# Linear attention of a four-layer trunk: its six projections as seven products of halves each

## The chip, the cores and the metric

One core of a Trainium2 chip runs the kernel. The metric is the device time of one execution in microseconds, as the median of several runs. A core has TensorE (in the profile PE for matmuls, PEld for loading the stationary operand), VectorE (DVE), ScalarE (ACT), GpSimd (POOL) and SyncE (SP). Each takes its instructions in order. SP and POOL also issue the DMAs; only POOL issues those that add to what is already in SBUF.

## The reference, cut to what matters

The model has four layers (S5, linear attention, differential attention, S5) of width 1024 over 512 tokens, each followed by a feed-forward. The change touches the second layer's mixer:

```python
def gla_mixer(h, w_in, w_a2, b_a, norm_g, w_o):
    proj = h @ w_in                                   # 512 x 1024 @ 1024 x 3088
    q, k, v, g, a_lo = jnp.split(proj, [512, 1024, 2048, 3072], axis=-1)
    log_a = jax.nn.log_sigmoid((a_lo @ w_a2 + b_a).astype(f32)) / GLA_TEMP
    cum = jnp.cumsum(log_a.reshape(shp_k), axis=2)    # chunks of 64 tokens, 4 heads
    tot = cum[:, :, -1]
    k_dec = k * jnp.exp(tot[:, :, None] - cum)
    upd = jnp.einsum('bnchk,bnchv->bnhkv', k_dec, v)
    state = dec_c[..., None] * state + upd_c          # scan over 8 chunks
    o = jnp.einsum('bnchk,bnhkv->bnchv', q, states)
    o = o * lax.rsqrt(jnp.mean(o * o, axis=-1, keepdims=True) + NORM_EPS) * norm_g
    o = o * jax.nn.silu(g)
    return o @ w_o
```

`h` is the RMS norm of x; x + mixer goes on to the feed-forward. All is in float32.

## The kernel before, in words

**Products.** Every large product runs as three matmuls of 32-bit parts: an operand is split into a rounded high part (a cast on ScalarE, line 414) and the low rest (a subtraction on VectorE, line 422), and high x high, high x low and low x high are added (`mm3`, lines 442 to 444). A weight arrives by DMA in a buffer `wst` (three of them) and is split into `whl` (five).

**Feed-forward.** Its first product runs in blocks of 512 columns by a scheme of seven products of halves (`seven_block`): tokens and contraction are halved, sums of the quarters of the activations ("sides" 1, 2, 3, 4, and the plain quarters 11, 12, 22; class `Sides`) and of the weights (1, 21, 22, 3) are formed, and each product is 2 x 4 x 3 matmuls that are 256 wide (line 585). Products six, seven and four add to the PSUM bank of product one, and three to that of five, after ScalarE or VectorE has read what stands there; two has a bank of its own. Sums of weights are made by a DMA that adds (POOL) and by VectorE (line 678). The first two blocks of a layer, in which the sides are made too, follow a plan written out as a list of steps; for it the order of all engines is by hand (`hand_all`). Elsewhere only TensorE's order is by hand, the order of the program (`hand(PE)`), and the other engines' instructions are put in order by a scheduler, by the order of the program among those that it holds ready.

**Linear attention** (`gla`, line 1903). The activations come as `Left`: eight transposed tiles with high and low parts. The six projections of 512 columns are plain products with 512-wide matmuls: q by `gemm_a4`, then in this order v (first half), k, v (second half), gate (first half), gate (second half), each by `gemm_b`. A `gemm_b` takes four weight pieces of two 128-row tiles; between pieces it calls functions given in `between`. These hold the rest of the work: `decays` (four 512-wide matmuls z, then on ScalarE absolute value, exponential and logarithm, lines 1970 to 1972), `later` (suffix sums, line 1977, and their exponential), `totals` (32 matmuls with two columns, line 1984), and for each half `hf` of the heads and token tile `t` `updates` (line 2007, then VectorE makes two states for each of two heads, line 2017) and `readout` (line 2031, ScalarE's sums of squares, line 2037, a power on POOL, line 533, and the scaled output, line 2045). An update of tile t stands one piece ahead of its readout. `turned` transposes the gated output (line 2062) and splits it (lines 538, 539). The output projection adds to x (line 566) and hands the rows to the next norm (lines 94, 107, 116).

## Time and profile before

| | |
|---|---|
| median of 3 runs (lowest, highest) | 2259.85 us (2259.85, 2261.8) |
| the profiled execution: its time, its span | 2262.09 us, 2260.1 us |
| linear attention's own matmuls, first projection to next layer's first product | 579.5 to 800.5 us of the span |
| HBM read, mean over the span | 285.62 MB; 134 GB/s with what is written |

The profile comes from one execution with a recorder running; a mean duration of an instruction is not its spacing, since matmuls and also the other engines' instructions overlap a little with the next. "Idle before" names what released an engine. A row "L2007 PE MATMUL upd<-v,kd" reads: line 2007, TensorE, a matmul that writes `upd` from `v` and `kd`.

### The profile page before, as it was taken

The page shows a single profiled execution, that of the slowest core. Times are in us where ns is not written, and L with a number is a line of the kernel's source. Part 1 is how long each engine was busy: PE and PEld are TensorE (multiplying, and loading weights), DVE is VectorE, ACT ScalarE, POOL GpSimd, SP SyncE. Part 2 cuts the span into 40 slices and gives each one's busy share as a digit, 9 for nine tenths or more (in the row PEclk, how much of TensorE's full clock was granted, in tenths as well). Part 3 has the DMA queues.
Part 4 walks back from the last instruction along what each step waited for, and adds up shares of the span by engine and source line. Part 5 has one row for each costly group of instructions (what it writes and reads, how often), then busy time and mean ns, then how long its engine had stood idle before and what let it go on. Part 6 is the DMA issues. An engine that isn't in the chain of part 4 may idle for free.

```text
span 2260.1 us, 37368 instructions
## 1 busy us (share of the span) xinstructions
PE 2185.5 (97%) x14967; PEld 1957.2 (87%) x14967; DVE 1578.0 (70%) x2415; ACT 1111.5 (49%) x1777; POOL 318.1 (14%) x432
## 2 busy tenths in 40 slices
PE   6999999999999999999999999999999899999998
PEld 5888889989777799998988888989999788989997
DVE  9955878776535488777745676976766965957675
ACT  8534635444443356564435675644544234635443
POOL 4301141430000010100002231101000000101000
PEclk9999999999999999999999999999999999999999
DMA  4356666663322566665346465975641545766622
GB/s 90 63 172 167 163 169 174 174 179 94 106 75 69 150 157 178 180 174 153 94 142 149 96 154 136 242 207 138 177 95 56 145 154 149 197 167 158 169 75 75
DMA packets 295527, 319.92 MB, mean 142 GB/s; under 512 B 70141, under 2 KB 235289, under 8 KB 295226
## 3 DMA queue, kind: packets, MB, share of 16 engines
q1 hardware_dynamic: 232730, 235.79, 34.2%
q0 software_dynamic: 62624, 81.75, 19.4%
q8 instruction: 118, 1.93, 0.3%
q14 instruction: 55, 0.45, 0.1%
HBM read 285.62 MB, written 16.65 MB: 134 GB/s over the span
## 4 chain that ended last, share of the span: by engine, by line
PE 83%; DVE 7%; ACT 4%; issue 3%; DMA 2%; SPq 1%; POOL 0%; DVEq 0%; POOLq 0%; ACTq 0%
PE a L585 17%; PE acc L442 13%; PE acc L444 13%; PE acc L443 13%; PE c L585 9%; PE d L585 5%; PE y L1490 2%; DVE whl L422 2%; ACT whl L414 1%; PE op L2332 1%; PE s L2299 1%; PE tp L116 1%; PE V L1454 1%; PE acc L2387 1%; DMA wst<-in_ffn_w_down_dram 1%
## 5 line engine op out<-in xcount | busy, mean ns | idle before, releaser
L422 DVE TENSOR_TENSOR whl<-wst,whl 128x1024 fp32r<-128x1024 f32 x272 | 331.7, 1224 | 277.8 <-ACT whl L414 276.7
L414 ACT CAST whl<-wst 128x1024 fp32r<-128x1024 f32 x272 | 284.9, 1052 | 339.7 <-PE acc L444 250.3
L585 PE MATMUL a<-side,whl 128*128 128x256 f32 x3168 | 382.5, 277 | 7.7 <-DVE whl L422 6.0
L585 PEld LDWEIGHTS a<-side,whl 128*128 128x128 f32 x3168 | 369.4, 188 | 10.1 <-DVE whl L422 6.8
L442 PE MATMUL acc<-whl,act 128*128 128x512 f32 x704 | 276.1, 392 | 1.9 <-DVE g L629 1.8
L444 PE MATMUL acc<-whl,act 128*128 128x512 f32 x704 | 274.5, 390 | 0.0
L443 PE MATMUL acc<-whl,act 128*128 128x512 f32 x704 | 274.5, 390 | 0.0
L585 PE MATMUL c<-side,whl 128*128 128x256 f32 x2112 | 254.7, 277 | 3.8 <-DVE whl L422 3.8
L585 PEld LDWEIGHTS c<-side,whl 128*128 128x128 f32 x2112 | 246.6, 188 | 4.8 <-DVE whl L422 4.6
L422 DVE TENSOR_TENSOR whl<-slot,whl 128x1024 fp32r<-128x1024 f32 x105 | 127.8, 1222 | 66.3 <-ACT whl L414 66.2
L442 PEld LDWEIGHTS acc<-whl,act 128*128 128x128 f32 x704 | 132.1, 188 | 31.4 <-DVE g L629 2.7
L444 PEld LDWEIGHTS acc<-whl,act 128*128 128x128 f32 x704 | 132.2, 188 | 27.7
L443 PEld LDWEIGHTS acc<-whl,act 128*128 128x128 f32 x704 | 132.2, 188 | 26.2
L414 ACT CAST whl<-slot 128x1024 fp32r<-128x1024 f32 x105 | 110.0, 1053 | 90.8 <-PE acc L444 46.3
L585 PE MATMUL d<-sides,whl 128*128 128x256 f32 x1056 | 129.2, 278 | 2.5 <-ACT whl L414 2.5
L585 PE MATMUL a<-sides,whl 128*128 128x256 f32 x1056 | 129.1, 278 | 1.8 <-DVE whl L422 1.2
L442 PE MATMUL acc<-whl,hT 128*128 128x512 f32 x320 | 129.1, 403 | 0.0
L585 PEld LDWEIGHTS d<-sides,whl 128*128 128x128 f32 x1056 | 124.8, 188 | 3.3 <-ACT whl L414 3.3
L585 PEld LDWEIGHTS a<-sides,whl 128*128 128x128 f32 x1056 | 124.9, 188 | 3.1 <-DVE whl L422 1.4
L443 PE MATMUL acc<-whl,hT 128*128 128x512 f32 x320 | 125.9, 393 | 0.0
L444 PE MATMUL acc<-whl,hT 128*128 128x512 f32 x320 | 125.8, 393 | 0.0
L620 POOL DMA_DIRECT2D wst<-in_ffn_w_gate_up_dram x44 | 57.0, 1296 | 443.2 <-DMA wst<-in_ffn_w_gate_up_dram 178.0
(456 smaller groups left out, 3938.1 us busy)
## 6 DMA issues: line engine op xcount, KB each, us to landing
wst<-in_ffn_w_gate_up_dram SPq DMA_DIRECT2D x88, 512.0 KB, 4.5
wst<-in_ffn_w_down_dram SPq DMA_DIRECT2D x88, 512.0 KB, 4.6
slot<-in_ffn_w_gate_up_dram SPq DMA_DIRECT2D x69, 512.0 KB, 6.2
wst<-in_ffn_w_gate_up_dram POOLq DMA_DIRECT2D x44, 512.0 KB, 6.0
halves<-in_ffn_w_gate_up_dram SPq DMA_DIRECT2D x42, 512.0 KB, 5.6
wst<-in_s_w_glu_dram SPq DMA_DIRECT2D x32, 512.0 KB, 5.0
wst<-in_gla_w_in_dram SPq DMA_DIRECT2D x24, 512.0 KB, 3.6
wst<-in_diff_w_qkv_dram SPq DMA_DIRECT2D x24, 512.0 KB, 3.9
```

The source lines that it names most:

```text
L116: tr.nc.tensor.transpose(p[:, j], h[:, j * P : (j + 1) * P], tr.ident[:])
L414: self.last["high"] = self.nc.scalar.copy(hl[:, 0], w[:])
L422: self.last["low"] = self.nc.vector.tensor_tensor(hl[:, 1], w[:], hl[:, 0].bitcast(F32), op=ALU.subtract)
L442: mm(out, lh, rh, start=first, stop=False)
L443: mm(out, lh, rl, start=False, stop=False)
L444: self.last["mm"] = mm(out, ll, rh, start=False, stop=last)
L585: mm(o, hl[:, x, k, c], row(y, k), start=first and not (j or k or n), stop=k == 3 and n == 2, skip_group_check=True,)
L620: nc.gpsimd.dma_start(w[:], left.quarter(*plus, b), accum_op=ALU.add)
L1454: mm(V[kk][z][:, bs(b)], inm[:, z, bs(b)], U[:, bs(b)], start=True, stop=True)
L1490: mm(yb[:, b], q[:, j, b], om[:, j // 2, bs(b)], start=False, stop=j == 3)
L2299: nc.tensor.matmul(ss[m][:], qs[:, m, ts], ks[:, m, z], start=z == 0, stop=z == 1)
L2332: nc.tensor.matmul(op[:, 0], aT[:, kt], vall[0][:, kt, j * P : (j + 1) * P], start=kt == 0, stop=kt == 3)
```

## The change

The six projections run as six blocks of seven products. Blocks 0 and 1 (q, first half of v) follow a plan like that of the feed-forward, blocks 2 to 5 (k, second half of v, the two gate halves) the function `block`, in which the former `between` functions stand between products. q is turned as before (weights stationary); the other five have the activations stationary (`held`). Each result is put together out of quarters by ScalarE copies and VectorE sums (`Turned`, `Rows`). The first feed-forward ends with `Sides` in place of `Left`. x is written to DRAM in two parts, its SBUF room is lent as `work` (the low-rank tile, scratch and the states, kept now as a ring of three token tiles), and x is read back behind the last readout. `la` (the log decays) and the second half of v share a room, as do others. `planned` only carries the loop over a plan's steps. Lines left out are marked by "...".

```diff
+GLA_COLS = (0, 1024, 512, 1536, 2048, 2560)
...
-    def seven_product(self, row, w, bank, first, hl=None):
+    def seven_product(self, row, w, bank, first, hl=None, held=False):
...
+                    two = (row(x, k)[:, c], hl[:, y, k]) if held else (hl[:, x, k, c], row(y, k))
                     mm(
-                        o, hl[:, x, k, c], row(y, k), start=first and not (j or k or n),
-                        stop=k == 3 and n == 2, skip_group_check=True,
+                        o, *two, start=first and not (j or k or n), stop=k == 3 and n == 2, skip_group_check=True,
+    def seven_quarters(self, slots, left, b, held, out, dbank):
...
+        def load(name, q, half, plus=None, room=None):
+            if name in ("11", "3"):
+                W[name] = self.staged(left.quarter(q, half, b), 4, 256)
+            else:
+                W[name] = slots.pop(0) if room is None else room
+                if room is not None:
+                    lent.add(name)
+                nc.sync.dma_start(W[name][:], left.quarter(q, half, b))
+            if plus:
+                nc.gpsimd.dma_start(W[name][:], left.quarter(*plus, b), accum_op=ALU.add)
+        def done(name):
+            if name not in lent:
+                slots.append(W[name])
...
+        def one():
+            bank["a"] = self.acc("a")
+            product("11", "11", bank["a"], True)
+        def one_out():
+            out.copy(0, 0, bank["a"])
+        def two():
+            bank["d"] = dbank("d")
+            product("12", "21", bank["d"], True)
+        def two_out():
+            out.plus(0, 0, bank["d"])
+            out.done(0, 0)
+        def five():
+            bank["c"] = self.acc("c")
+            product("1", "1", bank["c"], True)
+        def five_out():
+            out.copy(1, 1, bank["c"])
+        def add(name):
+            v.tensor_tensor(W["1"][:], W["1"][:], W[name][:], op=ALU.add)
+            done(name) if name == "21" else None
+        def six():
+            product("2", "1", bank["a"], False)
+        def six_out():
+            out.copy(0, 1, bank["a"])
+        def seven():
+            product("3", "3", bank["a"], False)
+        def seven_out():
+            out.minus(1, 1, bank["a"])
+            out.done(1, 1)
+        def three():
+            product("4", "22", bank["c"], False)
+            done("22")
+        def three_out():
+            out.less(0, 1, bank["c"])
+            out.done(0, 1)
+        def four():
+            product("22", "1", bank["a"], False)
+            done("1")
+        def four_out():
+            out.copy(1, 0, bank["a"])
+            out.done(1, 0)
...
+                    if l == 0:
+                        nxt = Sides(self, after, None, i["gla_w_in"][0], lambda half, b: GLA_COLS[b] + half * 256)
...
+                                ahead=(lambda: self.gla_ahead(nxt)) if tail and l == 0 else None,
+                                middle=(lambda: nxt.total("3")) if tail and l == 0 else None)
...
+    def gla_ahead(self, left):
+        self.xkept = self.dp.tile([SEQ, D], F32, name="xgla")
+        left.ahead(2)
+        self.nc.gpsimd.dma_start(
+            self.xkept[:].rearrange("(t p) c -> p t c", p=P)[:, :, :512], self.x[:, :, :512]
+        )
     def gla(self, l, left, after):
...
+        xd = self.xkept[:].rearrange("(t p) c -> p t c", p=P)
+        with self.tc.tile_pool(name="gla", bufs=1, reuse_waits="tile") as p:
+            room = lambda tag, name: p.tile([P, 4, 512], F32, tag=tag, name=name)
+            lent = [room(tag, "lent") for tag in "AB"]
+            left.open(p, ("1", "2", "3"))
+            v0 = room("C", "v0")
+            left.open(p, ("4", "22"))
+            lent.append(room("D", "lent"))
+            qT = room("Q", "qT")
+            on = [None, room("N", "on1")]
+            ng = p.tile([P, D], F32, name="ng")
             mask = p.tile([P, P], F32, name="mask")
+            ind = p.tile([P, 2], F32, name="ind")
+            dec = p.tile([P, NT, 4, 2], F32, name="dec")
+            walr = p.tile([P, KT, 32], F32R, name="walr")
+            wals = p.tile([P, 4, 32], F32R, name="wals")
+            nf = p.tile([P, NT], F32, name="nf")
+            fac = left.r
...
+            class Rows:
+                def __init__(_, to, then=None):
+                    _.to, _.then = to, then
+                def each(_, th, half, ps):
+                    for j in range(2):
+                        t = 2 * th + j
+                        yield t, _.to[:, t, half * 256 : half * 256 + 256], ps[:, j * 256 : j * 256 + 256]
+                def copy(_, th, half, ps):
+                    for t, o, y in _.each(th, half, ps):
+                        nc.scalar.mul(o, y, fac[:, t : t + 1])
+                def stt(_, th, half, ps, f, op):
+                    for t, o, y in _.each(th, half, ps):
+                        v.scalar_tensor_tensor(o, y, f[:, t : t + 1], o, op0=ALU.mult, op1=op)
+                def plus(_, th, half, ps):
+                    _.stt(th, half, ps, fac, ALU.add)
+                def minus(_, th, half, ps):
+                    _.stt(th, half, ps, nf, ALU.add)
+                def less(_, th, half, ps):
+                    _.stt(th, half, ps, fac, ALU.subtract)
+                def done(_, th, half):
+                    if _.then:
+                        _.then(slice(2 * th, 2 * th + 2), slice(half * 256, half * 256 + 256))
+            whole = lambda y: y[:].rearrange("p a b -> p (a b)")
+            parts = [whole(y)[:, n : n + 1024].rearrange("p (k n) -> p k n", n=256) for y in lent for n in (0, 1024)]
+            slots = [left.g[:].rearrange("p (k n) -> p k n", n=256)]
+            f = [
+                self.seven_quarters(slots, left, 0, False, Turned(), self.sbank),
+                self.seven_quarters(slots, left, 1, True, Rows(v0), self.sbank),
+            ]
+            f[0]["room21"](parts[0])
+            f[0]["room1"](parts[1])
+            f[1]["room21"](parts[2])
+            f[1]["room1"](parts[3])
+            f[0]["room22"](parts[4])
+            f[0]["summed"]()
+            f[1]["summed"]()
+            f[1]["room22"](parts[5])
+            wal = self.wp.tile([P, KT + 4, 16], F32, tag="wst", name="wal", bufs=3)
+            nc.sync.dma_start(wal[:, :KT], w[:, 3072:3088].rearrange("(a p) n -> p a n", p=P))
+            nc.sync.dma_start(ng[:], i["gla_norm"][0].partition_broadcast(P))
+            nc.gpsimd.dma_start(xd[:, :, 512:], self.x[:, :, 512:])
...
+            plan = """
+                split21a one:a split21b square flush one:b total1 one_out:a finish high1 low1 total2 split1a high2 low2
+                negative one_out:b two:a two:b split1b high3 two_out:a five:a add22a highSa two_out:b lowSa five_out:a
+                five:b add22b highSb diag lowSb low3 split3a six:a spread five_out:b rows six:b six_out:a split3b seven:a
+                six_out:b total4 split22a high4 low4 seven:b seven_out:a split22b three:a seven_out:b gates
+                add21a high22 low22 three:b highFa add21b lowFa highFb lowFb four:a four:b three_out:a three_out:b
+                four_out:a four_out:b
+            """
+            more = {"square": lambda: left.square(NT - 1, 1), "flush": self.flush, "gates": gates, "negative": negative}
+            self.planned(plan, left, f, more)
...
+            self.hand(mybir.EngineType.PE)
+            work = self.xp.tile([P, NT, D], F32, tag="x", name="work")
+            flat = whole(work)
+            aT, wa2 = flat[:, :512], flat[:, 512:1024]
+            ring = flat[:, :3072].rearrange("p (s z c n) -> p s z c n", s=3, z=2, c=2)
+            turn = [0]
+            def T():
+                turn[0] += 1
+                return flat[:, 3072 + turn[0] % 2 * 512 :][:, :512]
...
+            ap_ = self.sbank("alo")
+            sums = [(walr[:, k], "11" if k < 4 else "12", k % 4) for k in range(KT)]
+            sums = [sums, [(walr[:, k], "1", k) for k in range(4)] + [(wals[:, k], "22", k) for k in range(4)]]
+            for th in range(2):
+                for n, (a, side, k) in enumerate(sums[th]):
+                    for z in range(2):
+                        nc.tensor.matmul(
+                            ap_[:32, th * 256 : th * 256 + 256], a, left.row(side, z, k),
+                            start=not (th or n or z), stop=n == KT - 1 and z == 1, skip_group_check=True,
+                        )
+            v.tensor_tensor(aT[:32], ap_[:32], R[:32], op=ALU.mult)
             for h in range(4):
+                v.scalar_tensor_tensor(qT[:, h], qT[:, h], 128.0 ** -0.5, R[:], op0=ALU.mult, op1=ALU.mult)
+            kd = room("A", "kd")
+            on[0] = room("B", "on0")
+            la = room("D", "la")
...
-                    nc.scalar.activation(kd[:, t], row(bank), AF.Exp, scale=1.0 / 16.0)
+                    e = T()
+                    nc.scalar.activation(e, row(bank), AF.Exp, scale=1.0 / 16.0)
+                    v.tensor_tensor(kd[:, t], kd[:, t], e, op=ALU.mult)
...
+            vs = [v0, None]
+            st = lambda hf, z, ch: ring[:, (4 * hf + ch // 2) % 3, z, ch % 2]
...
+            def block(b, out, between):
+                between = iter(between)
+                s = self.seven_quarters(slots, left, b, True, out, self.acc)
+                for y in ("direct", "room1", "room22", "room21", "summed"):
+                    s[y]()
+                def step(*names):
+                    for n in names:
+                        s[n]()
+                    next(between, lambda: None)()
+                step("one", "one_out")
+                step("five", "five_out")
+                s["add"]("22")
+                step("six", "six_out")
+                step("two", "two_out")
+                step("seven", "seven_out")
+                step("three", "three_out")
+                s["add"]("21")
+                step("four", "four_out")
+            def gated(hf, gs):
+                def then(ts, cs):
+                    nc.scalar.activation(gs[:, ts, cs], gs[:, ts, cs], AF.Silu)
+                    v.tensor_tensor(on[hf][:, ts, cs], on[hf][:, ts, cs], gs[:, ts, cs], op=ALU.mult)
+                return Rows(gs, then)
             def core(hf):
-                def after0():
-                    if hf:
-                        readout(0, 3)
-                    updates(hf, 0)
-                def after1():
-                    readout(hf, 0)
-                    updates(hf, 1)
-                def after2():
-                    readout(hf, 1)
-                    updates(hf, 2)
-                def after3():
-                    readout(hf, 2)
-                    updates(hf, 3)
-                return after0, after1, after2, after3
+                steps = [lambda: updates(hf, 0)]
+                for t in range(3):
+                    steps.append(lambda t=t: (readout(hf, t), updates(hf, t + 1)))
+                return steps + [lambda: readout(hf, 3)]
+            slots += left.freed()
             pause = lambda: None
-            values(0, (decays, pause, pause, later))
-            self.gemm_b(stat, w, KT, 512, evac_k, between=(totals,))
-            values(1, core(0))
-            part = lambda hf, z: oT[hf][:, z] if hf == 0 else oT[1][z][:].bitcast(F32R)
-            gated(0, core(1))
-            g = self.gain(after)
-            first = lambda: (readout(1, 3), turned(0, (0,)))
-            gated(1, (first, *(lambda t=t: turned(0, (t,)) for t in (1, 2, 3))))
-            oT[1] = [late("oT1"), late("oT1")]
+            block(2, Rows(kd), (decays, pause, pause, pause, pause, totals))
+            vs[1] = room("D", "v1")
+            block(3, Rows(vs[1]), (later, *core(0)))
+            g = []
+            block(4, gated(0, room("C", "gate0")), core(1))
+            self.x = self.xp.tile([P, NT, D], F32, tag="x", name="x")
+            nc.gpsimd.dma_start(self.x[:], xd)
+            oT = [[room("D", "oT0"), room("A", "oT0")], None]
+            part = lambda hf, z: oT[hf][z][:].bitcast(F32R)
+            turns = [pause] + [lambda t=t: turned(0, (t,)) for t in range(NT)]
+            block(5, gated(1, room("C", "gate1")), turns)
+            oT[1] = [room("Q", "oT1"), room("B", "oT1")]
```

187 lines of the change are left out of this document (97 added, 90 removed).

## The prediction

> **What bounds the kernel now.** First the page: TensorE is busy for nearly the whole span, and the chain that ended last is mostly TensorE.
>
> ```profile
> span 2260.1 us, 37368 instructions
> PE 2185.5 (97%) x14967; PEld 1957.2 (87%) x14967; DVE 1578.0 (70%) x2415; ACT 1111.5 (49%) x1777; POOL 318.1 (14%) x432
> ...
> PE 83%; DVE 7%; ACT 4%; issue 3%; DMA 2%; SPq 1%; POOL 0%; DVEq 0%; POOLq 0%; ACTq 0%
> ```
>
> The change works in one stage, the linear attention (about 579 to 801 us). There I asked for the waits of TensorE and then for its engines by stretch (columns: PE, PEld, DVE, ACT, POOL busy, clock, DMA share, GB/s).
>
> ```profile
> PE acc L444 <- DVE oT L539: 1.0, 2, 0.7
> PE tp L116 <- DVE hh L94: 0.8, 1, 0.8
> ```
> ```profile
> 612.00:635.00 23.00, 23.00 (x89) 16.39 (x88) 6.35 (x7) 22.69 (x28) 0.00 (x0) 1.00 0.12 31
> 676.00:700.00 24.00, 24.00 (x128) 17.19 (x128) 11.21 (x24) 8.92 (x20) 2.09 (x3) 1.00 0.22 66
> ```
>
> TensorE waits 1.8 us in 222: it alone sets the time, and only fewer matmul columns shorten the stage. But two helpers are nearly unused (VectorE 11.2 of 24 us), while ScalarE is full from 612 to 635 (22.69 of 23). That costs nothing now, because TensorE has 22 us of products that ask nothing of ScalarE. Whether this stays so is the question.
>
> **The products (removed work).** A 512-wide matmul of line 442 to 444 starts every 0.227 us: 24 of them lie between the first row and the third. A 256-wide product of 24 matmuls (line 585) takes 2.72 us, from start to start of the last two rows.
>
> ```profile
> 606.38 0.39 PE L442 MATMUL acc<-whl,hT 128*128 128x512 f32 x1
> ...
> 611.83 3.60 PE L1968 MATMUL z<-wa,aT 128*128 128x512 f32 x8
> 614.87 0.80 PE L442 MATMUL acc<-whl,hT 128*128 128x512 f32 x1
> ```
> ```profile
> 877.50 2.88 PE L585 MATMUL c<-side,whl 128*128 128x256 f32 x24
> 880.22 2.88 PE L585 MATMUL a<-side,whl 128*128 128x256 f32 x24
> ```
>
> (611.83 - 606.38) / 24 = 0.227; half as wide, 2.72 / 24 = 0.1133, exactly half. Before, one 512-column projection is 8 x 4 x 3 = 96 wide matmuls, 21.8 us. After, it is 7 x 24 = 168 narrow ones, 19.04 us. Six projections: 6 x 2.72 = **-16.3 us**. The low-rank matmuls keep their columns (16 wide become 32 narrow). [...]
>
> **The head, written out by hand.** Blocks 0 and 1 (q and the first half of v) run by a copy of the feed-forward's opening plan, which the trace has for the layer after: one wait in its 14 products.
>
> ```profile
> 836.91 5.50 PE L585 MATMUL a<-side,whl 128*128 128x256 f32 x46 [1.73 <-DVE whl L422]
> ```
> ```profile
> 441.40:460.60 19.20, 19.20 (x171) 19.20 (x170) 16.22 (x19) 11.29 (x15) 1.29 (x1) 1.00 0.67 174
> ```
>
> Here VectorE leaves out that plan's two gate scalings, so I take **+0.5 us**, bounds 0 and twice the row, 3.5. The weights now come in 7 loads of 512 KB per block instead of 4. The second row is such a block of the first feed-forward, also with five weight slots: TensorE has no gap there at 174 GB/s, so the loads are hidden. The half of x that POOL writes to DRAM stands ahead of the sums of blocks 0 and 1 in POOL's fixed order and waits for x; the other half stands ahead of the norm's power but is ready before it. I price both, and the reading back during block 5 (due only after block 5 and half an output projection, over 40 us), at nothing; uncovered, 2 MB at the 174 GB/s above would be 12 us.
>
> **The decays (block 2).** They are the same ScalarE work as before (groups of lines 1971 and 1972, a square of the core for its shape, and the order of the chain):
>
> ```profile
> L1971 ACT ACT_TABLE_LOAD x4 | 5.1, 1283 | 0.1
> L1972 ACT ACT_TABLE_LOAD x4 | 5.1, 1283 | 0.1
> ```
> ```profile
> L2037 ACT ACTIVATE e<-op 128x256 f32<-128x256 f32 x16 | 6.0, 381 | 1.2 <-DVE on L2070 0.8
> ```
> ```profile
> 613.03 0.59 ACT L1970 ACTIVATE e<-z 128x512 f32<-128x512 f32 x1
> ...
> 615.47 0.58 ACT L1970 ACTIVATE e<-z 128x512 f32<-128x512 f32 x1
> 616.06 1.28 ACT L1972 ACT_TABLE_LOAD   x1
> ...
> 630.00 0.63 ACT L1972 ACTIVATE e<-e 128x512 f32<-128x512 f32 x1
> 630.53 1.98 ACT L414 CAST whl<-wst 128x1024 fp32r<-128x1024 f32 x2
> ```
>
> Eight table loads make it a chain of 630.63 - 613.03 = 17.6 us, and two weight casts that were due stand behind it at 630.53. Before, the next result that ScalarE had to take out of PSUM came 22 us later. In block 2 the chain is started behind product "one", and the copy six_out must empty bank a before product "seven" may add to it. Between them TensorE has z (614.87 - 611.83 = 3.04) and "five", "six", "two" (3 x 2.72), 11.2 us of cover from z's start. The chain starts 1.2 us after z (613.03 - 611.83) and ends at 18.8; six_out follows, two copies of a quarter each. Their shape (128x256) is that of the squares in line 2037, 0.38 each. So seven starts at about 19.2 to 20.3: a gap of **8 us** (bounds: 5.5, if the copy slips in ahead of the last logarithm, and 11, if five_out and two casts stand first too). I take 8, where only the chain stands first.
>
> A gap that long also costs clock:
>
> ```profile
> 645.00:650.00 5.00, 5.00 (x13) 3.91 (x12) 0.00 (x0) 0.00 (x0) 0.00 (x0) 0.50 0.22 85
> ```
> ```profile
> 1765.67 2.59 PE L1490 MATMUL y<-out,prods 128*128 128x128 f32 x8 [2.58 <-DVE prods L1481]
> ```
> ```profile
> 1766.00:1768.00 2.00, 1.79 (x8) 1.34 (x7) 2.00 (x5) 0.00 (x0) 0.00 (x0) 0.65 0.03 9
> 1768.00:1770.00 2.00, 2.00 (x12) 2.00 (x11) 2.00 (x5) 0.00 (x0) 0.00 (x0) 0.50 0.00 0
> ```
>
> After a gap of 2.58 us the clock was halved for some 3.4 us ((1 - 0.65) / 0.5 x 2 = 1.4, and 2), a loss of **1.7 us**. After the 32 two-column matmuls of the totals it was halved for all of 645 to 650 and a little more: up to 3.3 lost; both bound this term (0 to 3.3). [...] The loss behind the totals stays in both kernels.
>
> **The core (blocks 3 and 4).** Each of eight steps is a readout, an update and a product. In the order of the trace:
>
> ```profile
> 683.65 1.08 PE L2031 MATMUL op<-st,qT 128*64 128x256 f32 x8
> 684.66 1.13 PE L2007 MATMUL upd<-v,kd 64*128 64x256 f32 x8
> ```
> ```profile
> 684.83 1.22 DVE L422 TENSOR_TENSOR whl<-wst,whl 128x1024 fp32r<-128x1024 f32 x1 [3.58 <-ACT whl L414]
> 685.98 0.16 DVE L531 TENSOR_SCALAR ms<-ms 128x2 f32<-128x2 f32 x1
> 686.05 0.47 DVE L2017 SCALAR_TENSOR_TENSOR st<-st,dec,upd 128x256 f32<-128x256 f32 x1
> 686.95 0.88 DVE L2045 SCALAR_TENSOR_TENSOR on<-op,rs,ng 128x256 f32<-128x256 f32 x2 [0.43 <-POOL rs L533]
> 687.74 1.26 DVE L2017 SCALAR_TENSOR_TENSOR st<-st,dec,upd 128x256 f32<-128x256 f32 x3
> ```
>
> The update ends at 685.79 and its last state at 689.00, 3.2 us later. The next readout came 5.4 us later and never waited. Now it comes 2.72 us later; its last matmuls start another 0.8 on, so it just meets the state if VectorE does nothing else. But VectorE has more: per block 7 splits and 2 sums at about 1.15 (684.83 to 685.98), six quarters of 0.44 out of PSUM (0.88 / 2, same shape): 13 us, where 4 splits were 4.6. With 16 states of 0.42 (1.26 / 3), 8 outputs of 0.44, four sums of 0.16 and the wait on POOL (4 x 0.43) = 12.6, and four products or gates near 0.6, a block is 28 us. TensorE has 19.04 + 4 x 2.14 = 27.6, and 3 more in block 3 for the suffix sums. So VectorE is as long as TensorE in block 4. Neither waits as long as the weights are split up to five products ahead; each sum that falls between costs about 0.7. I take **+2.5 us**; bounds 0 and 8 (1 us in each step).
>
> POOL adds another wait: its powers (line 533) now stand in one queue with the summing DMAs, each of which holds the queue until the plain load lands.
>
> ```profile
> POOL slot L620 <- DMA slot<-in_ffn_w_gate_up_dram: 23.8, 2, 16.4
> ```
>
> Behind such a one wait the power, then VectorE's output, then the states, then TensorE's readout. Two or three of these DMAs fall between the powers; **+1 us**, bounds 0 and 5 (two that come 2.5 late). Loads are issued a block ahead, which speaks for the low end.
>
> **Block 5 and the end.** The first half is turned during block 5 with two products still to come, so the first wait of line 539 goes:
>
> ```profile
> 752.80 0.50 PE L444 MATMUL acc<-whl,oT 128*128 128x512 f32 x1 [0.67 <-DVE oT L539]
> ```
>
> **-0.7 us.** The norm's transposes, the totals and the output projection are the same work; the wait of line 116 (0.8) stays late as it is.
>
> **The sum.** -16.3 - 0.7 + 0.5 + 8 + 1.7 + 2.5 + 1 = **-3.3 us**. The profiled execution took 2262.1 us (span 2260.1 and 2.0 around it) and would take 2258.8. It lies 2.2 over the median of the runs, 2259.85, so I predict 2256.5. With every term at its low end it would be -11.5, with every one at its high end +13.8; I leave out that many high ends together.
>
> **The rivals.**
> 1. *The decays stay hidden.* Then 8 and 1.7 go: -13.0, 2246.8 us. For it: in the rows of the chain the second Abs (615.47) stands ahead of the first logarithm (its load at 616.06), so later work can slip between two dependent steps, and six_out might stand earlier. Against it: both casts due in that time stood behind the whole chain.
> 2. *The core becomes bound by VectorE and POOL* (the slower side). If the state is late by 1 us in each of eight steps and POOL by 5 in all, +13 stands for the +3.5 taken: 6.2 us slower than before, 2266.1. It decides from the point where a step's VectorE work exceeds its 4.86 us on TensorE (2.72 + 2.14); worked out above it is some 28 / 27.6 in block 4. For it: the in-order wait on POOL within each step. Against it: five splits ahead as a cushion.
> 3. *The narrow products do not keep their pace* beside so much copying, so that the change does not do what it says: without the 16.3 the rest is 13 us slower, 2272.9. Against it stands the full block at 441 to 461.
>
> **How the numbers follow.** Forecast (gap in block 2, cheap core; -8 to +1): 0.45; rival 1: 0.20; rival 2: 0.30; rival 3: 0.05. A measurement of this kernel tells about 0.2%, 4.5 us, from no change. Of the forecast's 0.45 a little less than half lies below -4.5; with rival 1 faster has 0.40. The rest of it and the edge of rival 2 give 0.27 for no change, and 0.33 is left for slower. The range reaches from just beyond rival 1, 2246.5, to somewhat past rival 2, 2268.5. The forecast alone spans 2252 to 2261.
>
> **What would show it.** Right: matmuls of line 442 to 444 down by 576 and of line 585-like ones up by 1008; in block 2 a TensorE gap of 6 to 10 us that ends with ScalarE's copy out of bank a, and a clock of 0.5 behind it; readouts waiting under 1 us each for states; VectorE over 90% busy in blocks 3 and 4. Wrong: no gap in block 2 (rival 1), readout waits of 1 us and more in most steps, released by VectorE or behind a POOL DMA (rival 2), products longer than 2.72 us at full clock (rival 3), or TensorE waiting for loads in the head, which I put at nothing.

## The result, and the profile after

| | before | after |
|---|---|---|
| median of 12 runs each (lowest, highest) | 2260.64 us (2258.18, 2262.54) | 2260.14 us (2256.48, 2261.69) |
| ratio to before, 95% interval | | 0.9996 [0.9987, 1.0005] |
| the profiled execution: its time, its span | 2262.09, 2260.1 | 2260.43, 2258.7 |
| from the first projection's first matmul to the output projection | 169.83 | 165.57 |

The change makes no difference that can be measured; the prediction had given that 0.27, behind 0.40 for faster and 0.33 for slower. The forecast of 2256.5 us was 3.6 us too low; for the profiled execution the sum gave 2258.8 and 2260.4 was measured. Several terms were wrong, in both directions.

The page of the changed kernel, its lines on engines and on the chain:

```profile
PE 2180.6 (97%) x15415; PEld 1978.1 (88%) x15415; DVE 1633.5 (72%) x2487; ACT 1142.9 (51%) x1837; POOL 338.9 (15%) x447
...
PE 79%; DVE 8%; ACT 5%; issue 4%; DMA 3%; SPq 1%; POOL 1%; DVEq 0%; POOLq 0%; ACTq 0%
```

TensorE has 448 matmuls more, as it should: 1008 narrow for 576 wide, and 16 more of the low rank. Its busy time fell by only 4.9 us. TensorE's waits in the linear attention (577 to 744 us):

```profile
PE a L592 <- ACT kd L2100: 3.5, 1, 3.5
PE op L2269 <- DVE work L2256: 0.7, 1, 0.7
PE a L592 <- DVE whl L426: 0.2, 1, 0.2
```

The first is the foreseen gap in block 2, at half the size. ScalarE in that block, then TensorE's row behind the gap, then two stretches of the view by window (PE, PEld, DVE, ACT, POOL busy, clock, DMA share, GB/s; clock is the granted clock as the profile shows it, 1 for TensorE's full speed):

```profile
627.57 1.09 ACT L2213 ACTIVATE work<-z 128x512 f32<-128x512 f32 x2
628.67 1.28 ACT L2214 ACT_TABLE_LOAD   x1
...
631.13 1.28 ACT L2215 ACT_TABLE_LOAD   x1
...
638.79 1.15 ACT L2215 ACTIVATE work<-work 128x512 f32<-128x512 f32 x2
639.85 0.46 ACT L2100 ACTIVATE kd<-c,rcol 128x256 f32<-128x256 f32 x1
640.20 0.83 ACT L2100 ACTIVATE kd<-a,rcol 128x256 f32<-128x256 f32 x2
```
```profile
641.09 5.49 PE L592 MATMUL a<-whl,side 128*128 128x256 f32 x24 [3.47 <-ACT kd L2100]
646.38 3.17 PE L592 MATMUL c<-whl,side 128*128 128x256 f32 x24
```
```profile
637.00:646.00 9.00, 5.53 (x29) 5.33 (x28) 4.43 (x6) 8.11 (x11) 0.00 (x0) 0.66 0.54 104
652.00:660.00 8.00, 8.00 (x57) 8.00 (x57) 4.17 (x4) 3.85 (x6) 0.00 (x0) 0.79 0.55 92
```

Each function is applied to two tiles at a time, so the chain has four table loads, not eight, and takes 639.94 - 627.57 = 12.4 us. Behind the gap the seventh product took 5.29 us from start to start at the lowered clock.

A second loss has no gap at all. Three products of the head, one after another:

```profile
604.59 2.89 PE L592 MATMUL a<-whl,side 128*128 128x256 f32 x24
607.31 2.99 PE L592 MATMUL c<-side,whl 128*128 128x256 f32 x24
610.14 2.99 PE L592 MATMUL c<-whl,side 128*128 128x256 f32 x24
```

The first starts 2.72 us before the next, like the rows that the prediction took from the feed-forward; the second 2.83, at a granted clock shown as 1. Taken matmul by matmul, the starts lie either 0.113 or 0.118 us apart, and which of the two holds changes only where a product begins. Of the 42 products 32 run at 0.118 and 8 at 0.113 (the two others at half clock); 713 of 965 spacings within products are the slower ones, 3.3 us in all. In the kernel before, the 512-wide matmuls of the stage keep to 0.227 in most of their spacings in every group (but for those at half clock behind the totals). Its narrow matmuls do not all keep to 0.113: of the 308 narrow products in its feed-forwards 25 run at 0.118, among them one 22 us ahead of the full block that the prediction took for rival 3:

```profile
419.40 2.99 PE L585 MATMUL a<-sides,whl 128*128 128x256 f32 x24
422.23 2.99 PE L585 MATMUL c<-side,whl 128*128 128x256 f32 x24
```

A third loss sits in the core. VectorE, POOL and TensorE around one step:

```profile
678.55 0.47 DVE L2256 SCALAR_TENSOR_TENSOR work<-work,dec,upd 128x256 f32<-128x256 f32 x1
680.07 0.88 DVE L2283 SCALAR_TENSOR_TENSOR on<-op,rs,ng 128x256 f32<-128x256 f32 x2 [1.05 <-POOL rs L539]
680.86 1.25 DVE L2256 SCALAR_TENSOR_TENSOR work<-work,dec,upd 128x256 f32<-128x256 f32 x3
```
```profile
677.96 1.33 POOL L624 DMA_DIRECT2D wst<-in_gla_w_in_dram  x1 [3.41 <-DMA wst<-in_gla_w_in_dram]
678.86 1.18 POOL L539 TENSOR_TENSOR rs<-ms,mhalf 128x2 f32<-128x2 f32 x1
```
```profile
681.39 1.46 PE L2269 MATMUL op<-work,qT 128*64 128x256 f32 x8
```

VectorE has made one state, then waits 1.05 us for POOL's power, which stands behind a summing DMA, and only after the two outputs come the other three states; the readout at 681.39 takes 1.46 instead of 1.08. The eight readouts took 11.2 us where they took 8.1 before; four of them were late, by 0.4 to 1.4 us. VectorE was not full, though:

```profile
663.00:695.00 32.00, 31.21 (x234) 25.31 (x232) 23.56 (x46) 13.43 (x32) 5.17 (x6) 1.00 0.42 90
695.00:719.00 24.00, 24.00 (x186) 19.32 (x185) 18.60 (x38) 12.98 (x30) 2.79 (x4) 1.00 0.22 67
```

That is 42.2 of 56 us, 75%.

**Where the time went**, from the starts of TensorE's matmuls in the two profiles (after minus before): ahead of the stage -1.8; the stage -4.3; output projection -0.7; feed-forward and differential attention behind it -0.4; third feed-forward **+4.6**; the rest +1.1; together -1.5, the difference of the spans. The third feed-forward and the rest hold no line that the diff touches. In the third feed-forward ScalarE stood waiting for the load of a weight, and the copy that TensorE needed stood behind that weight's cast:

```profile
1478.68 1.04 ACT L418 CAST whl<-wst 128x1024 fp32r<-128x1024 f32 x1 [4.21 <-DMA wst<-in_ffn_w_gate_up_dram]
1479.63 0.58 ACT L794 COPY r<-a 128x512 f32<-128x512 f32 x1
```

TensorE waited 3.2 us for that copy (0.3 in the profile of before), and its next two products took 3.0 us longer at a halved clock (0.84 on average from 1480 to 1500 us).

### The profile page after: what moved, and what is told of

It is laid out like the page before. It is cut to its first block, busy times and chain, and to the rows that moved or that the text cites. A ratio compares the mean times of both kernels' runs of the same rounds, so it can differ in the third digit from the quotient of the medians.

```text
span 2258.7 us, 38448 instructions
## 1 busy us (share of the span) xinstructions
PE 2180.6 (97%) x15415; PEld 1978.1 (88%) x15415; DVE 1633.5 (72%) x2487; ACT 1142.9 (51%) x1837; POOL 338.9 (15%) x447
## 4 chain that ended last, share of the span: by engine, by line
PE 79%; DVE 8%; ACT 5%; issue 4%; DMA 3%; SPq 1%; POOL 1%; DVEq 0%; POOLq 0%; ACTq 0%
PE a L592 19%; PE acc L446 11%; PE acc L448 11%; PE acc L447 11%; PE c L592 9%; PE d L592 5%; PE y L1618 2%; DVE whl L426 2%; ACT whl L418 1%; PE op L2571 1%; PE V L1582 1%; PE s L2538 1%; DMA wst<-in_ffn_w_gate_up_dram 1%; PE tp L117 1%; PE acc L2626 1%
## 5 line engine op out<-in xcount | busy, mean ns | idle before, releaser
L426 DVE TENSOR_TENSOR whl<-wst,whl 128x1024 fp32r<-128x1024 f32 x260 | 316.8, 1223 | 216.7 <-ACT whl L418 215.5
L418 ACT CAST whl<-wst 128x1024 fp32r<-128x1024 f32 x260 | 272.3, 1052 | 263.7 <-PE acc L448 175.1
L592 PE MATMUL a<-side,whl 128*128 128x256 f32 x3240 | 394.3, 278 | 9.9 <-DVE whl L426 6.2
L592 PEld LDWEIGHTS a<-side,whl 128*128 128x128 f32 x3240 | 380.6, 189 | 12.2 <-DVE whl L426 7.3
L592 PE MATMUL c<-side,whl 128*128 128x256 f32 x2160 | 261.0, 277 | 3.5 <-DVE whl L426 3.5
L592 PEld LDWEIGHTS c<-side,whl 128*128 128x128 f32 x2160 | 252.6, 188 | 4.4 <-DVE whl L426 4.3
L426 DVE TENSOR_TENSOR whl<-halves,whl 128x1024 fp32r<-128x1024 f32 x87 | 106.0, 1221 | 36.1 <-ACT whl L418 35.7
L418 ACT CAST whl<-halves 128x1024 fp32r<-128x1024 f32 x87 | 91.2, 1052 | 80.2 <-DVE halves L815 30.1
L859 ACT CAST act<-r 128x512 fp32r<-128x512 f32 (+1 forms) x110 | 66.2, 644 | 105.6 <-DVE r L840 85.1
```

The lines of the kernel that those rows point to most:

```text
L418: self.last["high"] = self.nc.scalar.copy(hl[:, 0], w[:])
L426: self.last["low"] = self.nc.vector.tensor_tensor(hl[:, 1], w[:], hl[:, 0].bitcast(F32), op=ALU.subtract)
L592: mm(o, *two, start=first and not (j or k or n), stop=k == 3 and n == 2, skip_group_check=True,)
L859: self.last["act high"] = nc.scalar.copy(dst[:, 0, j], src[:, j])
```

## The experiments

The ratios are to the kernel before, run beside them on the same chip; a gain "against the changed kernel" is against experiment 1. The expectations call experiment 8 r8, and so on.

**1. The changed kernel once more**, unaltered.

> The changed kernel once more, unaltered, as the measure for the others. Its first profile lost 4.6 us in the third feed-forward (1390 to 1753 us), which the change does not touch: TensorE waited 3.2 us for a weight there and then ran at a granted clock of 0.84 for 20 us. Theory A (the weight stream of that stage is at the limit of its DMA and scatters from execution to execution): this profile shows another wait there, anywhere from 0 to 4 us, and the profile of the kernel before scatters as much. Theory B (the changed kernel always loses there, since it comes to that stage earlier than its weights): a wait of 3 us or more again, followed by a lowered clock. Either way the ratio to the kernel before is 0.998 to 1.001.

Measured: 2259.53 against 2261.58 us, 0.9993 [0.9984, 1.0002]. The third feed-forward (from the last transposes of the attention before it to the first transposes of the scan behind it) took 362.05 us with 2.6 us of wait, so neither 364.3 nor 359.7: a part of the 4.6 us belonged to that one execution (the clock stayed at 1.00 this time), and a part came back. Theory A holds for the first part only; experiments 5, 9 and 10 take up the second.

**2. Narrow matmuls alone**, in the kernel before, for five of its six projections.

```diff
+        if getattr(self, "narrow", False):
+            for j in range(2):
+                c = slice(j * 256, j * 256 + 256)
+                mm(out[:, c], lh, rh[:, c], start=first and j == 0, stop=False, skip_group_check=True)
+                mm(out[:, c], lh, rl[:, c], start=False, stop=False, skip_group_check=True)
+                self.last["mm"] = mm(out[:, c], ll, rh[:, c], start=False, stop=last, skip_group_check=True)
+            return
...
+            self.narrow = True
...
+            self.narrow = False
```

> The kernel before, with nothing changed but that each 512-wide matmul of five of the six projections (values, keys, gates: 480 matmuls) is issued as two of 256 columns, 960 in all, with the same weights and the same sums. Theory A (narrow products are half as long as wide ones, as the sum of the prediction took it): 0 us, ratio 0.9995 to 1.0005. Theory B (between the core's small matmuls narrow ones fall to a start every 0.118 us instead of 0.1133, as most products of the changed kernel's linear attention did): 960 x 0.0045 = 4.3 us more, ratio 1.0015 to 1.0022, with the spacing seen in the rows between 644 and 750 us.

Measured: 2266.96 us, 1.0027 [1.0017, 1.0036]: some 6 us slower with the same columns. TensorE's rows between two readouts:

```profile
703.00 0.28 PE L445 MATMUL acc<-whl,hT 128*128 128x256 f32 x1
703.12 0.28 PE L446 MATMUL acc<-whl,hT 128*128 128x256 f32 x1
```

They start every 0.12 us, and so do 908 of 945 in the stage; 960 x (0.120 - 0.1133) = 6.4 us. Theory B's loss is there, and this stream is slower still than the changed kernel's. Its reason is not: 46 of the 47 spacings in the group from 605.55, which no small matmul interrupts, are 0.120 as well, so the core's small matmuls do not make it. In these traces a 256-wide matmul is half of a 512-wide one (0.227) at the faster spacing (0.113) alone, and not at 0.118 or 0.120.

**3. The decays grouped by function.** Four scratch buffers instead of two; all four Abs, then Exp, then Ln.

```diff
-                for t, bank in enumerate(four("z")):
...
-                    e = T()
-                    nc.scalar.activation(e, z, AF.Abs)
-                    nc.scalar.activation(e, e, AF.Exp, scale=-1.0)
-                    nc.scalar.activation(e, e, AF.Ln, bias=1.0)
+                es = [flat[:, 1024 + t * 512 :][:, :512] for t in range(NT)]
...
+                for e in es:
+                    nc.scalar.activation(e, e, AF.Exp, scale=-1.0)
+                for e in es:
+                    nc.scalar.activation(e, e, AF.Ln, bias=1.0)
```

> The changed kernel with the decays' steps grouped by function: four Abs, four Exp, four Ln, in four buffers instead of two, so that two table loads are left of the four that the trace shows between 627 and 640 us. Theory A (the gap of 3.5 us ahead of the seventh product of block 2 and the halved clock behind it are ScalarE's chain standing in front of one copy): the chain shrinks by 2 x 1.28 us and more, the gap goes below 1 us, the clock behind it stays at 1, and the kernel gains 3.5 + 2.5 = 6 us at most, 4 to 6 us, against the changed kernel (0.9975 of it). Rival B (the weight casts that follow the chain at 641 us are as late as the copy): the next product waits instead, and the gain is 0 to 2.5 us. Rival C (the lowered clock comes from elsewhere and stays): 2.5 to 3.5 us.

Measured: 2255.24 us, 0.9975 [0.9966, 0.9985]; 4.3 us under the changed kernel. ScalarE and TensorE in block 2:

```profile
627.81 1.58 ACT L2213 ACTIVATE work<-z 128x512 f32<-128x512 f32 x3
629.41 1.28 ACT L2215 ACT_TABLE_LOAD   x1
...
633.40 1.28 ACT L2217 ACT_TABLE_LOAD   x1
634.69 2.20 ACT L2217 ACTIVATE work<-work 128x512 f32<-128x512 f32 x4
```
```profile
638.39 3.09 PE L592 MATMUL a<-whl,side 128*128 128x256 f32 x24 [0.53 <-ACT kd L2100]
641.33 2.99 PE L592 MATMUL c<-whl,side 128*128 128x256 f32 x24
```

The chain takes 9.1 us (627.81 to 636.89), the gap is 0.5, and the seventh product runs in 2.94 us instead of 5.29. The stage is 5.4 us shorter (159.95 against 165.33). Theory A holds: gap and clock are one loss.

**4. The readout's outputs behind the states.** The two outputs that wait for POOL's power are issued after the next update.

```diff
...
+                def both(t):
+                    normed = readout(hf, t)
+                    updates(hf, t + 1)
+                    normed()
...
-                    steps.append(lambda t=t: (readout(hf, t), updates(hf, t + 1)))
...
+                    steps.append(lambda t=t: both(t))
```

> The changed kernel with one reordering in the core: VectorE's two outputs of a readout (which wait for POOL's power) stand behind the four states of the next update instead of in their midst. Theory A (the readouts' lateness, 11.2 us of matmuls where they took 8.1 before, is VectorE held up by POOL's power in front of three states): the readouts fall back to 8.1 to 8.6 us, 2.5 to 3 us gained against the changed kernel. Theory B (VectorE has too much to do in a step, whatever the order): less than 1 us gained.

Measured: 2256.57 us, 0.998 [0.9971, 0.9989], 3.0 us under the changed kernel. The same step on VectorE and TensorE:

```profile
679.23 1.65 DVE L2256 SCALAR_TENSOR_TENSOR work<-work,dec,upd 128x256 f32<-128x256 f32 x4
681.37 0.88 DVE L2285 SCALAR_TENSOR_TENSOR on<-op,rs,ng 128x256 f32<-128x256 f32 x2 [0.49 <-POOL rs L539]
```
```profile
681.93 1.08 PE L2269 MATMUL op<-work,qT 128*64 128x256 f32 x8
```

All eight readouts together take 8.1 us again. It was the order on VectorE, not the amount of its work: theory A. The stage is only 2.1 us shorter in this profile (163.21 against 165.33), since behind the totals the clock was halved for 6.8 us instead of 3.4; the last section says more on that.

**5. x's trip alone**, in the kernel before.

```diff
+            for c in (0, 512):
+                nc.gpsimd.dma_start(xd[:, :, c : c + 512], self.x[:, :, c : c + 512])
...
             gated(0, core(1))
+            nc.gpsimd.dma_start(self.x[:], xd)
```

> The kernel before, with x's trip alone: two stores of half of x to DRAM at the start of the linear attention and one load of the whole back into the same tile, 4 MB in all, and a DRAM tile of 2 MB that the changed kernel has too. Theory A (the trip lies beside other work, as the prediction took it): 0 us, 0.9995 to 1.0005; uncovered it would be up to 12 us in the linear attention. Theory B on the 2 us that the changed kernel's profiles lose in the third feed-forward (362.0 to 364.3 us from the last transposes of the attention before to the next scan, where the kernel before took 359.7 and 360.9), though every engine has the same instructions in the same order there: if it is the place of the DRAM tiles that moved, this kernel loses them too; if not, it takes some 360 us there.

Measured: 0.9996 [0.9988, 1.0005]. No cost of the trip shows. But here the load back was issued at 593.5 us, right behind the stores, and in the changed kernel at 718.3, beside block 5: that place was not tested by itself, and what speaks for it is that the changed kernel's profile has no TensorE wait there. The third feed-forward took 360.91 us with 1.2 us of wait, like experiment 2 without the tile (360.8): nothing points to the DRAM tile as the cause of the loss there. By chance the profile shows something about the clock: see the last section.

**6. The sixth product's copy on VectorE**, the chain on ScalarE left as it is.

```diff
+                        if _.to is kd and (th, half) == (0, 1):
+                            v.tensor_scalar_mul(o, y, fac[:, t : t + 1])
+                        else:
```

> The changed kernel with one copy moved: in block 2 the result of the sixth product leaves bank a by VectorE instead of ScalarE; the four table loads stay. Theory A (the gap is only this copy behind ScalarE's chain): no gap ahead of the seventh product, no halved clock behind it, the eighth then waits for weight casts that still stand behind the chain (they ended at 642.8 us, 2 to 3 us after the time at which it could start): 2 to 4 us gained against the changed kernel. Rival (the chain's casts are as late as the copy): less than 1 us gained, the gap stands one product later.

Measured: 2260.38 us, 0.999 [0.9981, 0.9998], like the changed kernel. VectorE, and TensorE's wait between 620 and 665 us:

```profile
636.34 0.48 DVE L2103 TENSOR_SCALAR kd<-a,rcol 128x256 f32<-128x256 f32 x1 [0.42 <-PE a L592]
640.99 1.29 DVE L2221 SCALAR_TENSOR_TENSOR la<-z,work 128x512 f32<-128x512 f32 x2 [4.16 <-ACT work L2220]
642.19 0.47 DVE L2103 TENSOR_SCALAR kd<-a,rcol 128x256 f32<-128x256 f32 x1
```
```profile
PE a L592 <- DVE kd L2103: 3.6, 1, 3.6
```

Neither theory foresaw it: the scheduler set one half of the copy ahead of `la` and the other behind it, and `la` waits 4.16 us for the same chain. The gap is still there, with another name in the wait. A copy that only changes engines can meet the same chain again through what stands ahead of it there.

**7. Both mended orders** (edits of 3 and 4).

> The changed kernel with both mended orders: the decays grouped by function and the readouts' outputs behind the states. If the two losses are separate, the gains add: 4.3 + 3.0 = 7.3 us under the changed kernel, near 2252.5 us, ratio to the kernel before 0.996. If one hides behind the other, 5 us or less.

Measured: 2251.47 us, 0.9954 [0.9941, 0.9967]; the stage takes 157.11 us, 8.2 less than in experiment 1. The gains add.

**8. The totals spread as well.** `totals` now takes the token tiles that it is to do.

```diff
...
-            block(2, Rows(kd), (decays, pause, pause, pause, pause, totals))
+            block(2, Rows(kd), (decays, pause, pause, pause, *(lambda ts=ts: totals(ts) for ts in ((0,), (1, 2), (3,)))))
```

> The kernel of the run before this with one more edit: the 32 matmuls of two columns, which stood together (3.5 us, and the granted clock halved behind them), are issued in three parts of 8, 16 and 8 between three products. Theory A (3.5 us of nearly idle TensorE is what lowers the clock; 0.9 and 1.7 us are too short for it): the spacing of the product behind them goes from 0.213 back to 0.113 to 0.118 us, 1.6 us gained. Rival (any interruption of this kind lowers it): no gain, some 0.2 us lost.

Measured: 2250.55 us, 0.9948 [0.9935, 0.9961]. The view by window from the first of these matmuls, and TensorE's rows:

```profile
641.00:649.00 8.00, 8.00 (x72) 8.00 (x71) 7.62 (x11) 2.00 (x2) 1.28 (x1) 1.00 0.47 131
```
```profile
641.13 0.95 PE L2235 MATMUL dps<-ind,la 128*128 128x2 f32 x8
641.94 3.07 PE L592 MATMUL c<-whl,side 128*128 128x256 f32 x24
```

The clock stays at 1 (in 11 and 12, which have this edit too, as well), no product is slowed by it, and the stage is 1.6 us shorter than in 7 (155.51). The whole shows 0.9 less, inside the scatter. This is the fastest of the study, 0.52% below the kernel before.

**9 and 10. The turn of the DMAs' semaphores**: in these traces SP's DMAs signal their end on eight semaphores in turn, and POOL's on eight others. Small loads that nothing reads shift that turn: one on POOL's queue and two on SP's in the changed kernel (below), seven and six in the kernel before.

```diff
...
+            for n in range(2):
+                nc.sync.dma_start(spare[:1, n : n + 1], i["gla_b_a"][0:1, n : n + 1])
+            for n in range(1):
+                nc.gpsimd.dma_start(spare[1:2, n : n + 1], i["gla_b_a"][0:1, n : n + 1])
```

> The changed kernel with three loads of 4 bytes more at the start of the linear attention (two on SP's queue, one on POOL's) into a spare tile that nothing reads. DMAs signal their end on eight semaphores in turn; with these three, every DMA after the stage has the semaphore that it has in the kernel before, where the changed kernel stands 6 (SP) and 7 (POOL) further. Theory A (the 2 us lost in the third feed-forward come from this turn): the stage takes 359.5 to 361 us, TensorE waits 0.3 to 1.5 us for the weight there, and the kernel gains 1 to 2 us. Theory B (they come from something else, such as the earlier start): 362 us and 2 us of waiting as in all seven profiles of the changed kernel and its variants; no gain.

> The kernel before with 13 such loads of 4 bytes (six on SP's queue, seven on POOL's), near the program's start, so that every DMA of the third feed-forward has the semaphore that it has in the changed kernel. Theory A: the third feed-forward takes 362 us and more, TensorE waits 2 us or more for the weight there. Theory B: 359.5 to 361 us, 0.3 to 1.5 us of waiting. The time of the whole: 0 to 2 us more by A, no change by B.

Measured: 0.9986 [0.9977, 0.9994] for 9 and 1.0007 [0.9998, 1.0016] for 10. The wait in the third feed-forward for the copy behind the late weight, in the first profile of the changed kernel, in 9 and in 10:

```profile
PE a L592 <- ACT r L794: 3.2, 1, 3.2
```
```profile
PE a L592 <- ACT r L794: 0.6, 1, 0.6
```
```profile
PE a L585 <- ACT r L657: 1.1, 1, 1.1
```

The third feed-forward took 360.73 us in 9, below every untreated profile of the changed kernel and its variants (361.6 to 364.3 in eight); that is theory A. It took 361.01 in 10, near the other three of the kernel before and its variants (359.7 to 360.9); that is theory B. Neither theory is the whole truth. In 9, 10 and 12, the three kernels with small loads, the rest of the span behind this feed-forward takes 508.5 to 509.4 us, in all others 506.7 to 507.8: the turn of the semaphores, or the loads themselves, moves time about, without a gain. Not settled.

**11. Halves alternating within a product** (on 8).

```diff
+        steps = [(j, k, n) for j in range(2) for k in range(4) for n in range(3)]
+        if held is not None:
+            steps.sort(key=lambda y: y[1:])
```

> The kernel of r8 with one edit: within each of the 42 products of the linear attention the two column halves of the bank alternate from matmul to matmul, instead of twelve to the one and then twelve to the other; the same 24 matmuls with the same operands. In r8, 34 of the 42 products start their matmuls every 0.118 us and 8 every 0.113. Theory A (the slower spacing hangs on twelve matmuls in a row into the same half, or on the order of the weights): the spacing changes, to 0.113 in most products (3 us gained) or to 0.120 and more in all. Theory B (it hangs on how a run of products is entered, not on their order within): some 34 and 8 again, no gain.

Measured: 2250.8 us, 0.9951 [0.9937, 0.9964]; 34 products at 0.118 and 8 at 0.113, nearly the same ones as in 8. The order of the halves within a product made no difference here.

**12. Experiment 8 with the loads of 9.**

> The kernel of r8 with the three small loads of r9. Theory A (the turn of the semaphores costs 1 to 2 us in the third feed-forward): the stage takes 360 to 361 us with less than 1.5 us of waiting for the weight, against 361.9 and 2.2 in r8, and the whole 1 to 2 us less than r8. Theory B: 362 us, 2 us and more of waiting, the same time as r8, 0.995 of the kernel before.

Measured: 2252.04 us, 0.9955 [0.9942, 0.9968]; the third feed-forward takes 361.29 us with 1.4 us of wait. It is a little shorter, the whole is not: no gain to be had there.

## Why the prediction was right in sum, and which of its terms were not

| term | predicted, us | measured, us | from |
|---|---|---|---|
| products by their columns | -16.3 | -16.3 | 1008 narrow for 576 wide |
| their spacing | 0 | +3.3 | 713 starts at 0.118 |
| head | +0.5 | +0.2 | the one wait |
| gap in block 2 | +8 | +3.5 | the wait |
| clock behind it, and behind the totals | +1.7 | +1.0 | +2.5 and -1.5 |
| core and POOL | +3.5 | +3.1 | readouts 11.2 against 8.1 |
| wait of line 539 | -0.7 | -0.7 | output projection 50.48 against 51.22 |
| low rank and totals | 0 | +0.1 | +0.5 and -0.4 |
| sum | -3.3 | -5.8 | |

The stage and the output projection together became 5.0 us shorter; the 0.8 between the sum and that is not assigned (the first matmuls of a product behind the core's small ones start late by 0.1). So **the stage gave more than forecast, and most of what it gave was lost again elsewhere.** That -5.0 lies near -3.3 is in part luck: the gap in block 2 was taken 4.5 us too long and the spacing 3.3 us too short, and the two nearly cancel. That the whole came out at no change is owed, as far as the profiles show, to the third feed-forward, for which the sum has no term.

**The products.** The failed step is "half as wide, 2.72 / 24 = 0.1133, exactly half". The rows were chosen from a stream that runs at the faster of two spacings, and the trace of before has the slower one too (the product at 419.40, with 2.83 us to the next, 0.118 a matmul). Experiment 2 shows the loss by itself. Rival 3 was this loss with too large a price: 3.3 us, not all 16.3; and it is not tied to "so much copying", since experiment 2 has it without the copies. Against the 0.1133 of the prediction, a narrow matmul took 4.5 ns more in most products, none in eight, and 6.7 in experiment 2.

**The decays.** The mechanism is as forecast, down to the instruction that ends the gap. The size failed at the step "Eight table loads make it a chain of 630.63 - 613.03 = 17.6 us": that was the order in the trace of before, where loads of both functions alternate tile by tile. The trace of after pairs the tiles, and four loads of 1.28 us fall away, 5.1 of the 5.2 us by which the chain is shorter. An order that a scheduler made for one program is not a property of the work. Experiment 3 shows the cause: with the grouping finished, gap and clock loss go.

**The clock.** Behind the gap it cost 2.5 us (5.29 for a product of 2.83), within the bounds of 0 to 3.3. That the loss behind the totals "stays in both kernels" was half right: 3.0 us before (96 wide matmuls in 24.8 us), 1.6 after.

**The core.** The sum of both terms, 3.5, was nearly met (3.1), but not for the reason of the larger one: 2.5 stood for VectorE as long as TensorE, over 90% busy, and VectorE was at 75%. What held the states was the in-order wait on POOL, priced at 1 and named for rival 2. Experiment 4 removes all of it without removing any work. Rival 2 did not decide: the two together stayed at 3.1 us, far from its 13.

**x's trip** shows no cost (experiment 5, with the load back at another place), and the wait of line 539 went as priced.

**The third feed-forward** is what the prediction had no term for. There the DMA is busy throughout: its share in the view by window is 1.00 and 1.07 from 1440 to 1480 us (1.07 and 1.12 in before), SP's loads into `wst`, `slot` and `halves` land in the median 9.8 to 12.9 us after their issue, and a weight that comes late stops TensorE, by way of ScalarE's copy, for 0.3 us in the first profile of before and 3.2 in that of after. The profiles of the changed kernel and its variants without small loads lie 0.7 to 4.6 us above those of the kernel before and its variants without small loads there. The engines' instructions behind the stage are the same and in the same order in both kernels. Neither the DRAM tile (experiment 5) nor clearly the turn of the semaphores (9 against 10) explains it. An earlier start of the stage doesn't either: in experiment 8 it begins 7.9 us earlier than in the first profile of after, and takes less, 361.87. It stays open.

## What to carry to other kernels

When work moves under another engine's cover, ask which copy frees the buffer that the next product writes and what stands ahead of it in its queue; grouping a chain by function, and issuing what feeds the critical engine ahead of what waits for a third one, gave 8 us here without removing any arithmetic. Take the price of a matmul from several stretches of the trace, and not from the smoothest alone: the slower spacing stood in the trace of before as well. And look for the gain once more behind the stage: here a later stage, whose weights come at a DMA share of 1.00 to 1.07, gave most of it back, for a reason that stays open.

## What the runs showed of the hardware

**Narrow matmuls started at three spacings in these traces**, at a clock shown as 1, for 256 columns: 0.113 us in 8 of the 42 products of the first profile of the changed kernel, 0.118 in 32 of them, and 0.120 in experiment 2 (908 of 945 starts). In the changed kernel the spacing changes where a product begins and then holds, through several products or for one. In the eight profiles of the changed kernel and of experiments 3, 4 and 6 to 9, 6 to 11 of the 42 products ran at 0.113, mostly the same ones. What sets it was not found.

**The 32 totals were followed by a halved clock in ten profiles, and not in an eleventh.** These are the profiles in which the totals stand together; the one with a full clock is experiment 5. First the window of before, then the rows and the window of experiment 5:

```profile
640.00:648.00 8.00, 8.00 (x44) 7.10 (x44) 1.23 (x1) 1.24 (x2) 0.00 (x0) 0.73 0.24 70
```
```profile
642.18 3.63 PE L1988 MATMUL dps<-ind,la 128*128 128x2 f32 x32
645.67 0.48 PE L442 MATMUL acc<-whl,hT 128*128 128x512 f32 x1
```
```profile
642.00:650.00 8.00, 8.00 (x53) 7.21 (x52) 1.23 (x1) 1.24 (x2) 0.00 (x0) 1.00 0.23 67
```

The totals cost 3.0 us of clock in before and nothing in experiment 5, where they took 3.49 us (645.67 - 642.18). They took as long in after and in experiment 3, where the clock was halved:

| profile | totals, from and to | their time, us | granted clock | over |
|---|---|---|---|---|
| experiment 5 | 642.18 to 645.67 | 3.49 | 1.00 | 642 to 650 |
| experiment 3 | 644.15 to 647.64 | 3.49 | 0.79 | 644 to 652 |
| after | 649.39 to 652.88 | 3.49 | 0.79 | 649 to 657 |
| before | 640.53 to 644.38 | 3.85 | 0.73 | 640 to 648 |
| experiment 10 | 639.79 to 644.37 | 4.58 | 0.83 | 640 to 660 |

So the time that the totals take does not tell experiment 5 from after. The trace's own record of the granted clock has it lowered from 643.63 to 650.46 in before and from 653.61 to 657.02 in after. In these two traces all recorded changes of the clock lie a whole number of steps of 3.413 us apart; in before it was lowered at 643.63 and 1766.61, 329 steps apart. Whether the place of the totals against such steps made the difference was not shown: no run moved the stretch on purpose. The spread totals of experiment 8, at most 1.7 us in one piece (644.85 to 646.55), left the clock at 1.
